# A two-layer decoder trunk on one core: gate and score orders, a three-block first gate load, and output weights taken early

## The chip, the core and the metric

The kernel runs on one core of a Trainium2 chip. A core has a matrix engine (TensorE, PE in the rows; PEld is its weight load), VectorE (DVE), ScalarE (ACT), GpSimd (POOL) and SyncE (SP), each with its own instruction queue that is worked off in order. Sixteen DMA engines move data for all of them. The metric is device time of the whole program in microseconds. A measurement of this kernel varies by about 0.2% (the three runs of before lie between 2964.33 and 2970.5 us).

## The reference

512 tokens of width 1024 pass two layers in float32. Layer 1 mixes tokens with gated linear attention (6 heads) and attention into 256 memory tokens; layer 2 with stick-breaking attention (12 heads) and the same memory attention. After each mixer comes an output projection, `x <- LN(alpha*x + mix)`, and then a product-key expert network (PEER), which holds most of the work:

```
s = einsum('nhpd,hpkd->nhpk', q, subkeys)            # 8 heads, 2 halves, 128 keys each
top_s, top_i = top_k(s, 16)                          # per half
best_s, best_pos = top_k(all 16*16 sums, 16)         # 16 experts of 16384 per token and head
g = softmax(best_s)
act = gelu(einsum('nd,nhkd->nhk', x, u_tab[idx]))
out = einsum('nhk,nhkd->nd', g * act, v_tab[idx])
x <- LN(alpha*x + out)
```

## The kernel before

Every float32 product is made of three fast ones: an operand is split into a high part (`hi`, ScalarE copy) and the rest (`lo`, VectorE subtraction), and TensorE adds hi·hi, hi·lo and lo·hi (`split` at L85, `stat_mm` at L106). A weight block of 128x1024 is loaded by SyncE's queue into one of four `raw` buffers, split into one of three `hl` buffers, and used for 24 matmuls.

Mixer A runs L395 to L640. The first blocks give the low-rank gate input `glr`; `gate_logits` (L444) multiplies it with a weight of 16 rows (tile `pz`) and takes Abs, Exp and Ln on ScalarE; keys, queries and values follow. `to_cat` (L547) transposes a head's result (tile `ptc`) and splits it into `cat`. `out_proj_ln` (L232) splits eight blocks of output weights (`woh`, `wol`), multiplies `cat` by them for four groups of 128 tokens (tile `oacc`), and normalizes. `warm_sqrt` (L917) is a one-element square root that loads ScalarE's table early. Mixer B (L647) ends in the same `out_proj_ln`; `phase3` and `phase4` are its last attention steps.

`peer` (L966) has two long phases for 384 of the 512 tokens. The first (U) makes 16 query blocks and their scores (`pq`, copied to `qT`, then `pss`; L1317 to L1350), then runs over 128 blocks of 128 experts: 24 matmuls give `ph`, ScalarE's Gelu gives the activations. All but the last KEEP=20 activations go to DRAM (`Ad`). Beside this, generators paced by a budget per block pick the experts of one token tile after the other (`rest`, L1288: `rows` is the top-k, then `indices`, `softmax`, `gate_prep`) and turn them into a dense gate matrix in DRAM (`Gd`). The other 128 tokens are handled by gathers: GpSimd fetches expert rows, VectorE multiplies (`gr`, `va`; stream `gus`).

The second phase (V) takes the experts in the order of `vorder`, the kept ones first: gate times activation gives `w` (L1423), split into `whi` and `wlo`, and 18 matmuls per block add into `acc`. Gates come from `Gd` in loads of several blocks. The first load has G0=1 block and lies in `big`, beside the kept activations; the second (3 blocks) lies in `xlo` and the third (8 blocks) in `xhi`, which are free only when the last matmul of U has read them. The later ones have 8 blocks and alternate between the two. All are issued by SyncE.

In U and V the order on PE, DVE and ACT is that of the code; in the mixers a scheduler orders ACT and DVE, and the code orders PE. A semaphore wait holds back all that stands behind it on that engine's queue, DMA issues included.

## Time and profile before

| | us |
|---|---|
| median of three runs | 2969.97 (2964.33 to 2970.5) |
| the profiled execution | 2965.86 |
| its span, first to last instruction | 2964.2 |
| TensorE busy | 2910.8 (98%) |
| VectorE busy | 2400.5 (81%) |
| ScalarE busy | 1429.6 (48%) |
| GpSimd busy | 640.8 (22%) |

Mixer A with its output projection fills the first 0.26 ms, PEER of layer 1 runs to 1.48 ms, mixer B to 1.75 ms, PEER of layer 2 to the end. TensorE has little idle time that the profile names, but a busy share says nothing about its clock: the columns of granted clock by stretch show where the engine worked at half speed. In the rows, `[1.63 <-ACT woh L98]` means that the engine sat idle for 1.63 us until ScalarE's instruction of line 98 was done.

### The profile page before, as it was taken

The page shows a single profiled execution, that of the slowest core. Times are in us where ns is not written, and L with a number is a line of the kernel's source. Part 1 is how long each engine was busy: PE and PEld are TensorE (multiplying, and loading weights), DVE is VectorE, ACT ScalarE, POOL GpSimd, SP SyncE. Part 2 cuts the span into 40 slices and gives each one's busy share as a digit, 9 for nine tenths or more (in the row PEclk, how much of TensorE's full clock was granted, in tenths as well). Part 3 has the DMA queues.
Part 4 walks back from the last instruction along what each step waited for, and adds up shares of the span by engine and source line. Part 5 has one row for each costly group of instructions (what it writes and reads, how often), then busy time and mean ns, then how long its engine had stood idle before and what let it go on. Part 6 is the DMA issues. An engine that isn't in the chain of part 4 may idle for free.

```text
span 2964.2 us, 44555 instructions
## 1 busy us (share of the span) xinstructions
PE 2910.8 (98%) x16274; PEld 2573.2 (87%) x16274; DVE 2400.5 (81%) x5301; ACT 1429.6 (48%) x2484; POOL 640.8 (22%) x560
## 2 busy tenths in 40 slices
PE   8999999999999999999999999999999999999998
PEld 7878899999998888888776788999999998888886
DVE  5556899999886888878967668999999778888888
ACT  5342357666674333333345523476676743333332
POOL 0100132221333222322002001312223233222220
PEclk9999999999999999999999999999999999999999
DMA  4331488889989999999511214888989999999995
GB/s 164 121 114 57 148 301 302 319 310 332 337 317 334 323 346 346 359 360 356 186 65 43 100 57 142 295 305 314 315 318 332 328 330 338 349 347 356 367 351 175
DMA packets 315132, 789.91 MB, mean 266 GB/s; under 512 B 41873, under 2 KB 134049, under 8 KB 308513
## 3 DMA queue, kind: packets, MB, share of 16 engines
q1 hardware_dynamic: 216960, 419.48, 41.1%
q0 software_dynamic: 73728, 268.47, 25.5%
q10 hardware_dynamic: 24224, 99.13, 8.5%
q8 instruction: 127, 2.08, 0.3%
q14 instruction: 93, 0.75, 0.1%
HBM read 692.09 MB, written 94.90 MB: 266 GB/s over the span
## 4 chain that ended last, share of the span: by engine, by line
PE 91%; DVE 6%; issue 1%; DMA 1%; ACT 1%; DVEq 0%; ACTq 0%; SPq 0%
PE ph L118 11%; PE ph L120 11%; PE ph L119 11%; PE acc L262 11%; PE acc L264 11%; PE acc L266 11%; PE pq L118 2%; PE pq L119 2%; PE pq L120 2%; PE pg L1274 1%; PE pg L1275 1%; PE pss L1322 1%; PE oacc L264 1%; PE oacc L266 1%; PE oacc L262 1%
## 5 line engine op out<-in xcount | busy, mean ns | idle before, releaser
L118 PE MATMUL ph<-xhi,uh 128*128 128x384 f32 x2048 | 700.7, 342 | 0.0
L120 PE MATMUL ph<-xhi,ul 128*128 128x384 f32 x2048 | 686.2, 335 | 0.2
L119 PE MATMUL ph<-xlo,uh 128*128 128x384 f32 x2048 | 685.3, 335 | 0.0
L98 ACT ACTIVATE vh<-vr 128x1024 fp32r<-128x1024 f32 x256 | 271.4, 1060 | 593.0 <-issue 401.3
L1002 POOL DMA_INDIRECT gr<-in_un,gidx x256 | 302.3, 1181 | 1010.7 <-DVE gr L1037 805.5
L262 PE MATMUL acc<-vh,whi 128*128 128x512 f32 x1536 | 474.8, 390 | 7.8 <-ACT whi L1426 7.8
L264 PE MATMUL acc<-vl,whi 128*128 128x512 f32 x1536 | 474.4, 390 | 0.0
L266 PE MATMUL acc<-vh,wlo 128*128 128x512 f32 x1536 | 473.7, 390 | 0.5 <-DVE wlo L1427 0.5
L1002 POOL DMA_INDIRECT gr<-in_vt,gidx x256 | 287.2, 1122 | 766.4 <-DVE va L1055 657.4
L99 DVE TENSOR_TENSOR vl<-vr,vh 128x1024 fp32r<-128x1024 f32 x256 | 313.2, 1224 | 170.3 <-ACT vh L98 170.0
L98 ACT ACTIVATE uh<-ur 128x1024 fp32r<-128x1024 f32 x288 | 304.6, 1058 | 245.3 <-PE ph L119 230.1
L99 DVE TENSOR_TENSOR ul<-ur,uh 128x1024 fp32r<-128x1024 f32 x288 | 350.0, 1216 | 68.0 <-ACT uh L98 65.2
L119 PEld LDWEIGHTS ph<-xlo,uh 128*128 128x128 f32 x2048 | 385.7, 188 | 0.0
L120 PEld LDWEIGHTS ph<-xhi,ul 128*128 128x128 f32 x2048 | 385.0, 188 | 0.8 <-DVE ul L99 0.8
L118 PEld LDWEIGHTS ph<-xhi,uh 128*128 128x128 f32 x2048 | 385.5, 188 | 0.0
L262 PEld LDWEIGHTS acc<-vh,whi 128*128 128x128 f32 x1536 | 288.0, 188 | 69.8 <-ACT whi L1426 10.4
L266 PEld LDWEIGHTS acc<-vh,wlo 128*128 128x128 f32 x1536 | 288.2, 188 | 61.7 <-DVE wlo L1427 2.2
L264 PEld LDWEIGHTS acc<-vl,whi 128*128 128x128 f32 x1536 | 288.3, 188 | 61.4 <-DVE vl L99 1.8
L1055 DVE SCALAR_TENSOR_TENSOR va<-gr,gw,va 128x1024 f32<-128x1024 f32 x254 | 324.8, 1279 | 13.1 <-DMA gr<-in_vt,gidx 12.8
L1037 DVE SCALAR_TENSOR_TENSOR gr<-gr,xnat 128x1024 f32<-128x1024 f32 x256 | 309.7, 1212 | 16.0 <-DMA gr<-in_un,gidx 15.9
L1247 ACT ACTIVATE obl<-obh,rat 128x128 f16<-128x128 f16 x768 | 244.3, 393 | 19.9 <-ACT gt L1278 6.1
L1426 ACT ACTIVATE whi<-w 128x384 fp32r<-128x384 f32 x256 | 130.9, 511 | 55.6 <-DVE w L1423 55.5
(332 smaller groups left out, 4136.5 us busy)
## 6 DMA issues: line engine op xcount, KB each, us to landing
ur<-in_ut SPq DMA_DIRECT2D x256, 512.0 KB
vr<-in_vt SPq DMA_DIRECT2D x256, 512.0 KB
Gd<-gt ACTq DMA_DIRECT2D x48, 1024.0 KB
gl<-Gd SPq DMA_DIRECT2D x30, 1536.0 KB
Ad<-act ACTq DMA_DIRECT2D x108, 384.0 KB
al<-Ad SPq DMA_DIRECT2D x108, 384.0 KB
ur<-in_wq SPq DMA_DIRECT2D x32, 512.0 KB
bs<-in_b_st SPq DMA_DIRECT2D x14, 512.0 KB
```

The costliest lines, as they stand in the source:

```text
L98: nc.scalar.activation(hi, raw, AF.Copy)
L99: sub = lambda: eng.tensor_sub(lo, raw, hi.bitcast(F32))
L118: nc.tensor.matmul(ps, h, xhi[:, c, sl], start=(c == 0), stop=False)
L119: nc.tensor.matmul(ps, h, xlo[:, c, sl], start=False, stop=False)
L120: nc.tensor.matmul(ps, l, xhi[:, c, sl], start=False, stop=(c == NC - 1))
L262: nc.tensor.matmul(acc[hf], lh, hi[:, hf * 512:(hf + 1) * 512], start=first, stop=False)
L264: nc.tensor.matmul(acc[hf], lh, lo[:, hf * 512:(hf + 1) * 512], start=False, stop=False)
L266: nc.tensor.matmul(acc[hf], ll, hi[:, hf * 512:(hf + 1) * 512], start=False, stop=last)
L1002: nc.gpsimd.indirect_dma_start(out=gr, out_offset=None, in_=tab, in_offset=bass.IndirectOffsetOnAxis(ap=gidx[:, k:k + 1], axis=0))
L1037: nc.vector.scalar_tensor_tensor(gr, gr, 1.0, E.x[:, 0], op0=ALU.mult, op1=ALU.mult, accum_out=gh[:, k:k + 1])
L1055: nc.vector.scalar_tensor_tensor(va, gr, gw[:, k:k + 1], va, op0=ALU.mult, op1=ALU.add)
L1247: nc.scalar.activation(obl[:, q], obh[:, q], AF.Copy, scale=rat[:, n0 + q:n0 + q + 1])
```

## The change

1. `gate_logits` yields after each of its three products, and one of them is made after each projection block instead of three in a row.
2. The output weights of mixer A's first two chunks, and of mixer B's first, are split before `out_proj_ln`, into buffers that are free by then (tags `za` and `zs`). The load of `x` for the first normalization is issued earlier.
3. `warm_sqrt` reads the LayerNorm weight `gam`, times zero, so it runs after that load has landed.
4. In the score loop the copy of a query block (`query`) is separated from its scores and made in the iteration in which the block is computed.
5. `rest` does one step of the next tile's top-k before `gate_prep` of the present one. The gather stream takes no step in the last two rounds of U.
6. KEEP goes from 20 to 18 and G0 from 1 to 3. The second gate load, now 7 blocks (3 to 9), is issued on ScalarE's queue; the third (10 to 17) stays on SyncE's.

The Python lines that carry the change (some buffer widths, and the buffer count of the LayerNorm's `lny`, are left out):

```diff
-def out_proj_ln(E, cat, wo, lng, lnb, ahead, order=range(NC), rows=None):
+def wo_split(E, wo, c, pool, tag="", rows=None):
+    return split(E, load_raw(E, wo[c], "wo"), "wo", pool, tag, rows=None if rows is None or c >= GH else rows[:, c:c + 1])
+def out_proj_ln(E, cat, wo, lng, lnb, ahead, order, w, rows=None):
...
     with E.tc.tile_pool(name="lp", bufs=1, reuse_waits="tile") as lp:
-        w = {}
         for c in order:
-            w[c] = split(E, load_raw(E, wo[c], "wo"), "wo", lp, f"wo{c}", rows=None if rows is None or c >= GH else rows[:, c:c + 1])
+            if c not in w:
+                w[c] = wo_split(E, wo, c, lp, f"wo{c}", rows)
         gam, bet = load_ln(E, lp, lng, lnb)
-        warm_sqrt(E)
+        warm_sqrt(E, gam)
         next(ahead)
...
     with tc.tile_pool(name="acat", bufs=1, reuse_waits="tile") as ap:
-        hgc = ap.tile([P, GH], F32, name="hgc")
+        hgc = ap.tile([P, 32], F32, name="hgc")
         kk = ap.tile([P, 8, T], F32, tag="kk", name="kk")
...
         cat[7] = c7[:, 0], c7[:, 1]
+        new_za = lambda name, shape=(2, T), dt=F32: ap.tile([P, *shape], dt, tag="za", name=name, bufs=4)
+        wo = {}
         for c in (4, 5):
...
             nc.scalar.dma_start(bgt, a["a_bg"])
-            nc.scalar.dma_start(hgc, a["a_hg"])
+            nc.scalar.dma_start(hgc[:, :GH], a["a_hg"])
             nc.gpsimd.memset(seg, 1.0)
...
                     nc.tensor.matmul(pz, w2[:, j], glr[:16], start=True, stop=True)
-                    za = wk.tile([P, 2, T], F32, tag="za", name="za", bufs=3)
+                    za = new_za("za")
                     zb, az = za[:, 0], za[:, 1]
...
                     zz.append((zb, az))
+                    yield
                 for zb, az in zz:
...
                 st = stat_units(E, wst, range(1, 9), ev_stat, name="as")
-                next(st)
-                gate_logits()
+                logits = gate_logits()
                 for _ in st:
-                    pass
+                    next(logits, None)
                 mhi, mlo = mem_split(E, mp, "mr", a["memT"])
...
                 mem = mem_attn(E, wk, qm, cat, lambda hh: wk.tile([P, NT, 256], F32, tag="S", name="mp"),
-                               lambda hh: wk.tile([P, 2, T], F32, tag="za", name="mpT", bufs=3), ptags=("ps", "ps", "ps"))
+                               lambda hh: new_za("mpT"), ptags=("ps", "ps", "ps"))
...
                 nc.gpsimd.tensor_copy(E.Vm, kv1[1])
+                nc.sync.dma_start(E.x, a["x"].rearrange("(t p) d -> p t d", p=P))
                 rg = mp.tile([P, NT, GH * P], F32, tag="mr", name="rg")
...
                 next(rs_)
+                for c in range(2):
+                    wo[c] = wo_split(E, a["a_wo"], c, lambda name: new_za(name, (D,), F32R), rows=hgc)
                 to_cat(2)
...
                     to_cat(h)
-                with tc.issue_after(E.last_load.ins):
-                    nc.sync.dma_start(E.x, a["x"].rearrange("(t p) d -> p t d", p=P))
         yield
-        out_proj_ln(E, cat, a["a_wo"], a["lng0"], a["lnb0"], E.ahead, [0, 1, 2, 3, 6, 7, 4, 5], hgc)
+        out_proj_ln(E, cat, a["a_wo"], a["lng0"], a["lnb0"], E.ahead, [0, 1, 2, 3, 6, 7, 4, 5], wo, hgc)
...
             new_cat(c)
+        new_zs = lambda name, n, dt=F32: cp.tile([P, n], dt, tag="zs", name=name, bufs=2)
         with tc.tile_pool(name="mbx", bufs=1, reuse_waits="tile") as mp, tc.tile_pool(name="mbwk", bufs=2, reuse_waits="tile") as wk:
...
                 for h in two:
-                    tiles[h] = (wk.tile([P, 1280], F32, tag="zs", name="zs", bufs=4),
+                    zs = wk.tile([P, 1280], F32, tag="zs", name="zs") if g % 4 else new_zs("zs", 1280)
+                    tiles[h] = (zs,
                                 wk.tile([P, 1280 + 3 * P], F32, tag="ez", name="ez", bufs=2))
...
                 phase3(11)
+                first = {0: wo_split(E, wo, 0, lambda name: new_zs(name, D, F32R))}
                 phase4(5)
         yield
-        out_proj_ln(E, cat, wo, lng, lnb, E.ahead, [0, 1, 2, 3, 4, 6, 7, 5])
+        out_proj_ln(E, cat, wo, lng, lnb, E.ahead, [0, 1, 2, 3, 4, 6, 7, 5], first)
...
-def warm_sqrt(E):
-    E.nc.scalar.activation(E.junk1, E.one1, AF.Sqrt)
+def warm_sqrt(E, after):
+    E.nc.scalar.activation(E.junk1, after[:, 0:1], AF.Sqrt, scale=0.0)
...
 T0 = T - TD
-KEEP = 20
+KEEP = 18
 KB = P - KEEP
...
 GD = 1
-G0 = 1
+G0 = 3
 VE = 8
...
             def rest():
+                prev = None
                 for k, t in enumerate(order):
...
                     sel = sels[k] if k < 2 else Sel(t)
-                    yield from sel.rows()
+                    rows = sel.rows()
+                    if prev:
+                        yield next(rows)
+                        yield from prev.gate_prep()
+                    yield from rows
                     yield from sel.indices()
                     yield from sel.softmax()
-                    yield from sel.gate_prep()
+                    prev = sel
+                yield from prev.gate_prep()
...
-            def scores(r, pq):
+            def query(pq):
                 qT = wk.tile([P, T], F32, tag="act", name="qT")
                 nc.scalar.activation(qT, pq, AF.Copy)
+                return qT
+            def scores(r, qT):
                 pss = psum(E, name="pss")
...
                 stat_mm(E, pes[r], *parts.pop(r), sl=LATE)
-            pq = None
+            qT = None
             for r in range(17):
...
                 if r > 0:
-                    ev = scores(r - 1, pq)
+                    ev = scores(r - 1, qT)
                 if r + 2 >= LEAD:
                     prep(r + 2)
+                if r < 16:
+                    qT = query(pn)
                 if r > 0:
                     ev()
-                pq = pn
                 if r > 1:
...
                     work(WB if ready else WB0)
-                gus(GU if work.q else GU2)
+                if b < P - 1:
+                    gus(GU if work.q else GU2)
                 if LOG:
...
         vorder = list(range(KB, P)) + list(range(KB))
+        def new_gates(i, i1):
+            return E.xp.tile([P, NSUB, i1 - i, TS], F32, tag=("xhi", "xlo")[gcuts.index(i) % 2], name="gl")
+        def load_gates(eng, dst, b, b1):
+            eng.dma_start(dst, Gd[:, :, b:b1].rearrange("s p i n -> p s i n"))
...
                     vp["g"] = g0
+                    load_gates(nc.sync, g0, b, b + g1)
+                elif i == G0:
+                    vp["g"] = vp.pop("second")
                 else:
-                    vp["g"] = E.xp.tile([P, NSUB, g1 - i, TS], F32, tag=("xhi", "xlo")[gcuts.index(i) % 2], name="gl")
-                nc.sync.dma_start(vp["g"], Gd[:, :, b:b + g1 - i].rearrange("s p i n -> p s i n"))
+                    vp["g"] = new_gates(i, g1)
+                    load_gates(nc.sync, vp["g"], b, b + g1 - i)
                 vp["i"] = i
...
             vprep(1)
+            vp["second"] = new_gates(G0, gcuts[2])
+            load_gates(nc.scalar, vp["second"], KB + G0, KB + gcuts[2])
             for b in range(P):
...
                     vp["ln"] = load_ln(E, wv, lng, lnb)
-                    warm_sqrt(E)
+                    warm_sqrt(E, vp["ln"][0])
                 gus(vb)
...
         if out_dram is None:
```

What stands where on the engines, before and after, at three places. A row is line, operation, written tile <- read tiles, shape; ACT, SP are queues worked off from top to bottom. Lines of after are those of the changed file.

**End of mixer A, ScalarE's queue.** `arh` and `rg` belong to the gated attention, `aT` and `sq` to a head's result, `cat` and `xhi` are what the output projection multiplies with, `woh` its weights, `uh` the first block of the expert network. Before, from the last transposes on:

```order
L192 ACTIVATE cat_1567<-ptc 128x512 x2
L609 ACTIVATE rg<-ara 128x256 x4
L192 ACTIVATE cat_1567<-ptc 128x512 x2
L192 ACTIVATE xhi<-ptc 128x512 x2
L101 ACTIVATE woh<-wo,hgc 128x1024 x4
L924 DMA gam<-in_lng 128x1024
L98 ACTIVATE woh<-wo 128x1024
L925 DMA bet<-in_lnb 128x1024
L98 ACTIVATE woh<-wo 128x1024
L101 ACTIVATE woh<-wo,hgc 128x1024 x2
L98 ACTIVATE uh<-ur 128x1024 x3
```

After, an earlier stretch (weights of the first two chunks):

```order
L100 ACTIVATE arh<-ar 128x1024
L194 ACTIVATE cat_102<-mo 128x512
L100 ACTIVATE arh<-ar 128x1024 x2
L103 ACTIVATE woh<-wo,hgc 128x1024
L100 ACTIVATE arh<-ar 128x1024
L103 ACTIVATE woh<-wo,hgc 128x1024
L100 ACTIVATE arh<-ar 128x1024
L543 ACTIVATE aT_608<-po 128x512
L545 ACTIVATE sq<-po 128x512
```

and from the last transposes on:

```order
L194 ACTIVATE cat_1567<-ptc 128x512 x2
L620 ACTIVATE rg<-ara 128x256 x4
L194 ACTIVATE cat_1567<-ptc 128x512 x2
L194 ACTIVATE xhi<-ptc 128x512 x2
L103 ACTIVATE woh<-wo,hgc 128x1024 x2
L100 ACTIVATE woh<-wo 128x1024 x2
L940 DMA gam<-in_lng 128x1024
L941 DMA bet<-in_lnb 128x1024
L103 ACTIVATE woh<-wo,hgc 128x1024 x2
L934 ACT_TABLE_LOAD
L934 ACTIVATE junk_70<-gam 128x1
L100 ACTIVATE uh<-ur 128x1024 x3
```

Two of the eight `woh` have moved ahead of the heads' results `aT` and `sq`; six remain behind the last `cat`, and the square root of `junk` now reads `gam`.

**Score loop, ScalarE's queue.** `qT` is the copy of a query block, `sall` that of its scores, `uh` the split of the next weights. Before:

```order
L1319 ACTIVATE qT<-pq 128x512
L98 ACTIVATE uh<-ur 128x1024
L1323 ACTIVATE sall<-pss 128x512
L1319 ACTIVATE qT<-pq 128x512
L98 ACTIVATE uh<-ur 128x1024
L1323 ACTIVATE sall<-pss 128x512
L1319 ACTIVATE qT<-pq 128x512
```

After:

```order
L1342 ACTIVATE qT<-pq 128x512
L100 ACTIVATE uh<-ur 128x1024
L1342 ACTIVATE qT<-pq 128x512
L1349 ACTIVATE sall<-pss 128x512
L100 ACTIVATE uh<-ur 128x1024
L1342 ACTIVATE qT<-pq 128x512
L1349 ACTIVATE sall<-pss 128x512
L100 ACTIVATE uh<-ur 128x1024
```

The copy `qT` of a block stands one weight split earlier: ahead of `sall` of the block before instead of behind it.

**Start of V, the queues that issue the gate loads.** `vr` are weight loads of V, `gl` gate loads (24x16 elements a block: 24x48 is three blocks, 24x112 seven, 24x128 eight). SyncE before, from the third-last weight load ahead of them:

```order
L86 DMA vr<-in_vt 128x1024 x3
L1411 DMA gl<-Gd 128x24x48
L1411 DMA gl<-Gd 128x24x128
L86 DMA vr<-in_vt 128x1024 x2
L1411 DMA gl<-Gd 128x24x128
L86 DMA vr<-in_vt 128x1024 x8
L1411 DMA gl<-Gd 128x24x128
```

SyncE after:

```order
L85 DMA vr<-in_vt 128x1024 x3
L1432 DMA gl<-Gd 128x24x128
L85 DMA vr<-in_vt 128x1024 x7
L1432 DMA gl<-Gd 128x24x128
L85 DMA vr<-in_vt 128x1024 x8
L1432 DMA gl<-Gd 128x24x128
```

ScalarE before (`keep` is an activation of the last blocks of U, `vh` a weight split of V, `whi` the high part of gate times activation):

```order
L98 ACTIVATE vh<-vr 128x1024
L1366 ACTIVATE keep<-ph 128x384
L1426 ACTIVATE whi<-w 128x384
L98 ACTIVATE vh<-vr 128x1024
L1366 ACTIVATE keep<-ph 128x384 x2
L1426 ACTIVATE whi<-w 128x384
L98 ACTIVATE vh<-vr 128x1024
L1426 ACTIVATE whi<-w 128x384
L98 ACTIVATE vh<-vr 128x1024
```

ScalarE after:

```order
L1393 ACTIVATE keep<-ph 128x384
L100 ACTIVATE vh<-vr 128x1024
L1393 ACTIVATE keep<-ph 128x384
L1463 ACTIVATE whi<-w 128x384
L100 ACTIVATE vh<-vr 128x1024
L1393 ACTIVATE keep<-ph 128x384
L1463 ACTIVATE whi<-w 128x384
L1432 DMA gl<-Gd 128x24x112
L1393 ACTIVATE keep<-ph 128x384
L100 ACTIVATE vh<-vr 128x1024
L1463 ACTIVATE whi<-w 128x384
```

The second gate load has left SyncE's queue, grown from three blocks to seven, and stands in ScalarE's behind the second `whi`; the load of eight blocks is now the first of the two in SyncE's queue. The first gate load lies outside these rows (earlier in SyncE's queue); it has three blocks instead of one.

## Rows read from the trace of the kernel before

**Rows 1.** Page: span, busy time, costliest group (busy, mean ns, idle before).

```profile
span 2964.2 us, 44555 instructions
...
PE 2910.8 (98%) x16274; PEld 2573.2 (87%) x16274; DVE 2400.5 (81%) x5301; ACT 1429.6 (48%) x2484; POOL 640.8 (22%) x560
...
L99 DVE TENSOR_TENSOR vl<-vr,vh 128x1024 fp32r<-128x1024 f32 x256 | 313.2, 1224 | 170.3 <-ACT vh L98 170.0
```

**Rows 2.** Waits of TensorE over the span: us in total, times, longest.

```profile
PE acc L262 <- ACT whi L1426: 7.8, 6, 4.5
...
PE pss L1322 <- ACT qT L1319: 4.7, 4, 1.2
PE gtp L1209 <- DVE best L1183: 3.8, 2, 1.9
```

**Rows 3.** Chain that ended last: start us, us, what.

```profile
15.70 0.23 PE asp L118
...
21.83 3.17 PE pz L447 x6
...
30.43 0.43 PE asp L118
...
145.58 1.02 PE pd L507 x28
...
200.58 7.28 DMA wo<-in_a_wo
...
939.05 7.62 DMA gl<-Gd
...
2427.01 5.85 DMA gl<-Gd
```

**Rows 4.** Stretches: busy by engine, then PEclk, DMA share, GB/s.

```profile
24.90:31.00 6.10, 6.10 (x16) 4.77 (x15) 1.04 (x2) 6.04 (x9) 0.00 (x0) 0.51 0.26 86
140.00:183.00 43.00, 42.99 (x367) 34.86 (x367) 14.49 (x43) 14.11 (x21) 9.71 (x5) 1.00 0.29 104
945.00:950.00 5.00, 2.14 (x5) 1.75 (x6) 3.30 (x5) 2.11 (x4) 0.00 (x0) 0.57 1.08 312
950.00:955.00 5.00, 5.00 (x18) 3.97 (x18) 5.00 (x7) 1.89 (x3) 2.60 (x1) 0.75 1.09 346
2092.50:2096.00 3.50, 3.50 (x13) 3.50 (x12) 3.20 (x8) 3.07 (x5) 0.11 (x1) 0.51 0.49 187
```

**Rows 5.** Timeline of TensorE, projection A: start, us, instructions [idle before].

```profile
193.64 0.33 PE L550 MATMUL ptc<-ident,aT 128*128 128x128 f32 x1 [1.07 <-DVE aT L544]
195.70 1.22 PE L262 MATMUL oacc<-woh,cat 128*128 128x512 f32 x2 [1.72 <-ACT woh L101]
...
210.97 0.63 PE L266 MATMUL oacc<-woh,xlo 128*128 128x512 f32 x2
```

**Rows 6.** Timeline of TensorE, projection B.

```profile
1680.42 2.37 PE L750 MATMUL pav<-zs,v 128*64 128x512 f32 x14 [0.41 <-ACT zs L742]
1684.41 0.73 PE L262 MATMUL oacc<-woh,cat 128*128 128x512 f32 x2 [1.63 <-ACT woh L98]
...
1697.69 0.62 PE L266 MATMUL oacc<-woh,cat 128*128 128x512 f32 x2
```

**Rows 7.** Timeline of TensorE, starts of V in both layers.

```profile
939.03 0.63 PE L262 MATMUL acc<-vh,whi 128*128 128x512 f32 x2
...
942.70 0.61 PE L266 MATMUL acc<-vh,wlo 128*128 128x512 f32 x2
947.86 1.22 PE L262 MATMUL acc<-vh,whi 128*128 128x512 f32 x2 [4.55 <-ACT whi L1426]
...
2434.05 0.73 PE L262 MATMUL acc<-vh,whi 128*128 128x512 f32 x2 [1.96 <-ACT whi L1426]
```

**Rows 8.** Timeline of ScalarE, middle of V in layer 1.

```profile
1207.85 0.34 ACTq L924 DMA_DIRECT2D gam<-in_lng  x1
...
1211.52 1.06 ACT L98 ACTIVATE vh<-vr 128x1024 fp32r<-128x1024 f32 x1 [1.06 <-issue]
```

More of the change, by code (lines that the diff above doesn't have):

```diff
@@ L49, in setup @@
     E.Vm = E.cp.tile([P, 2, 256], F32, name="Vm")
-    E.one1 = E.cp.tile([P, 1], F32, name="one1")
+    E.pad1 = E.cp.tile([P, 1], F32, name="pad1")
     E.junk1 = E.cp.tile([P, 1], F32, name="junk1")
-    nc.gpsimd.memset(E.one1, 1.0)
     E.zl = E.cp.tile([1, P], mybir.dt.bfloat16, name="zl")
@@ L94, in split @@
     pool = pool or E.hl
-    hi = pool.tile([P, D], F32R, tag=tag + "hi", name=f"{name}h")
-    lo = pool.tile([P, D], F32R, tag=tag + "lo", name=f"{name}l")
+    if callable(pool):
+        hi, lo = pool(f"{name}h"), pool(f"{name}l")
+    else:
+        hi = pool.tile([P, D], F32R, tag=tag + "hi", name=f"{name}h")
+        lo = pool.tile([P, D], F32R, tag=tag + "lo", name=f"{name}l")
     if rows is None:
@@ L404, in mixer_a @@
             w2 = mp.tile([16, 3, P], F32, name="w2")
-            bgt = mp.tile([P, 3], F32, name="bgt")
+            bgt = mp.tile([P, 16], F32, name="bgt")[:, :3]
             msk = mp.tile([P, P], mybir.dt.uint8, name="msk")
@@ L890, in layer_norm @@
     nc = E.nc
-    y = lp.tile([P, D], F32, tag="lny", name="lny", bufs=2)
+    y = lp.tile([P, D], F32, tag="lny", name="lny")
     st = E.lnp.tile([P, 2, 6], F32, tag="lnst", name="lnst", bufs=2)
```

## The prediction

> **What bounds the kernel now.** I read the page first. TensorE is busy for 2910.8 of 2964.2 us [rows 1], so nothing else can bound the whole, and the change adds no product. What it can win is the 53 us in which TensorE is idle, and the time in which it counts as busy at half clock. So I read next the waits of TensorE, which name three that the change touches [rows 2]; then the chain of waits, for places where a DMA ended last [rows 3]; then the granted clock of the stretches behind those places [rows 4]; and last the timelines of TensorE around both output projections and the starts of V [rows 5 to 7], where a matmul's start says more than a sum of idle time. The reader is to see there that the losses are short and lie at seams: none is over 5 us of idleness, and most are followed by some us at clock 0.5.
>
> Everything is summed against the profiled execution, 2965.86 us. It is 4.1 us below the median of the three runs shown, 2969.97; I set the prediction between both.
>
> **Part by part.** (1) *Gate logits.* The six products `pz` stand together and take 3.17 us [rows 3], with 16 rows of the array in use. Behind them the clock is 0.51 (1.2 of 2.4 GHz) for 24.9 to 31.0 us, and a matmul of `asp` takes 0.43 instead of 0.23 us [rows 3, 4]. About 6.1 / 0.43 = 14 matmuls run there, less the one at the seam: 13 x 0.20 = 2.6, and 0.3 for the step itself, 2.9 us lost. Spread out, each pair is about 1 us long. A stretch of 28 small products of 1.02 us in all [rows 3] lies in 140 to 183 us, whose clock is 1.00 [rows 4]: so much does not make it fall there. Breaking the projection two more times I put at 0.25 each. I take -2.4, with ends of -2.9 and, if each of the three makes the clock fall as the six did, 3 x 2.9 - 2.9 = +5.8. ScalarE's table changes that this brings are hidden: the logits are used only in the keys, many blocks later.
>
> (2) *Output projection of A.* The last `ptc` ends at 193.64 + 0.34 = 193.98, and the 48 matmuls of the first four tiles' share run until about 211.43 [rows 5]: 17.45 us for 48 x 0.23 = 11.0 of work. So 6.4 us can be had. Two chunks ready at the start give 12 matmuls, 2.8 us, of cover for the third, whose two splits are then under way. But the last weight load still waits for a buffer and takes 7.28 us to land [rows 3], beside `gam`, `bet` and now no longer `x`. I take -5.0; ends -6.4 and -1.7, the last being the first wait alone, 1.72 [rows 5].
>
> (3) *Scores.* `pss` waits 4.7 us for `qT`, four times [rows 2]. With `qT` ahead of `sall` and made in the iteration of its own block, it has the whole score group to get done. -4.5; ends -4.7 and 0.
>
> (4) *Gate transposes.* `gtp` waits 3.8 us for VectorE's softmax, twice, and the clock behind one is 0.51 for 3.5 us [rows 2, 4], of which half, 1.7, is lost. With one step of the next tile's top-k set between the softmax and the transposes the wait goes in both. -4.5; ends -5.5 and 0, if VectorE, which is then later with the next weights (`ul`), gives it back.
>
> (5) *Output projection of B.* `pav` ends at 1682.79, the first half of the projection at 1697.69 + 0.46 = 1698.15 [rows 6]: 15.36 for 11.04 of work, 4.3 to be had. Only one chunk is ready here, so a later one may be short: -3.0; ends -4.3 and -1.0.
>
> (6) *Start of V.* Layer 1 waits 4.55 us after its first block, as its second gate load lands only at 946.7, 7.62 us after its buffer came free [rows 3, 7]. The clock then falls to 0.57 and 0.75 [rows 4]: 0.43 x 2.14 + 0.25 x 5 = 2.2 lost. So 6.8 in all; layer 2 loses 1.96. Afterwards the first load covers three blocks. A block is 18 x 0.23 = 4.1 us [rows 7], so the fourth starts 12.3 us after 939.03, at 951.3, and VectorE and ScalarE need its gates 1.2 us before, at 950.1 (product and copy, the gap from 946.67 to 947.86). Its load has 24 x 112 x 4 x 128 bytes, 1.38 MB instead of 0.59, and cannot start before 939.05 either: `xlo` is read by the last product of U. It now runs beside the 1.57 MB of SyncE's eight-block load, not ahead of it, and beside two gathers of 0.52 MB. All four are 4.0 MB; at the 312 GB/s of [rows 4] they take 12.8 us, so it lands at 952 to 953 and TensorE waits 2 to 3 us, in both layers. With the clock behind it that is worth 2.7: layer 1 gains 4.1, layer 2 loses 0.8. I take -3. The ends: -8.8 if the load is in time, and +9.3 if it only gets the rate of the three-block load (0.59 MB in 7.62 us, 77 GB/s), as then it needs 17.8 us, lands at 956.9 and each layer loses 9.
>
> By the Trainium skill, page "DMA: Bandwidth & Descriptors", section "Issuing engines are not separate DMA queues", transfers issued by ScalarE, SyncE and GpSimd end on the same 16 engines and interleave, and issuing from several saves only the issue time. By that rule the two loads share the rate, as the sum above has them, and the move of the queue gains nothing and gives up the place ahead. Had ScalarE's queue engines of its own, the load would land about like the one of before, and term 6 would be -8.8. The row at 945 to 950, with every engine busy (DMA share 1.08), speaks for sharing.
>
> (7) *The square root.* In V it now waits for `gam`, and ScalarE's queue with it: the next `vh`, then `vl` on VectorE. That `vh` starts at 1211.52 and is multiplied two blocks later, 8.2 us; less 1.06 and 1.22 [rows 1, 8] 5.9 us are spare. `gam` is issued at 1207.85 [rows 8], so it may take 9.6 us to land. The landings shown take 5.85 to 7.62 us [rows 3]. I take 0; the end is rival 4.
>
> Two kept activations fewer mean two more to DRAM and back, 0.2 MB each way of 790 MB; the gather stream skips two rounds in U and has V to catch up, under TensorE's work. Both 0.
>
> Sum: -2.4 - 5.0 - 4.5 - 4.5 - 3.0 - 3.0 = -22.4. That is 2943.5 against the profiled execution, 2947.6 against the median; I say 2946.
>
> **The rivals.** *Seven blocks in time.* If the load of ScalarE's queue gets more than half of the rate, it lands by 950.1 and term 6 is -8.8: -28, 2939. For it speaks the 346 GB/s of the stretch behind [rows 4]; against it the queue's size.
>
> *A long wait at the fourth block.* If it gets the rate of the three-block load, term 6 is +9.3: -10, 2956. For it: that load too ran beside gathers and the eight-block one. Against it: that one was bound by what lay ahead of it at its start, and its rate need not hold for 1.38 MB.
>
> *Waits replaced.* The clock falls at each gate product (+5.8), or VectorE's late `ul` takes the place of the transposes' wait, and the third chunk of both projections is as late as the first was: -10 again, 2956. For it speaks that six products of 3.17 us did it once; against it the 1.00 over 43 us with such stretches [rows 4].
>
> *Slower: the square root holds V up.* ScalarE stands still until `gam` is there, and with it the splits of weights and gates. Up to 9.6 us nothing happens; beyond that each us costs one, in both layers. To use up 22.4 us it must take 9.6 + 11.2 = 20.8 us to land. At 25 us each layer loses 15.4 and some 2 of clock: +35, so +13 in all, 2979. For it: `gam` stands in a row with gathers that fill the engines all through V. Against it: loads of the same size landed in 6 to 8 us under that load.
>
> *Nothing moves.* The waits named are parts of 53 us of idleness, and each could be the front of another one, so that about nothing is left, 2966.
>
> **How the numbers follow.** Forecast 0.50, seven blocks in time 0.22, a long wait 0.15, waits replaced 0.08, square root 0.03, nothing 0.02. The range reaches from below the second case, 2933 (all terms near their good ends), to above the third and fourth, 2961. It leaves out the last two and the tails. Faster or slower counts from 0.2%, 6 us, about what a measurement of this kernel can tell: below 2964, within, above 2976. The forecast and its first three rivals, 0.95 together, lie below 2964; I leave 0.07 of that to their upper tails, so faster 0.88; same 0.08, six of those seven and the last case; slower 0.04, the square root and the rest.
>
> **What the new profile would show.** (1) `pz` in three pieces and clock 1.00 behind each; (3, 4) no `pss` and hardly a `gtp` among the waits; (2, 5) the first `oacc` within 0.5 us of the last `ptc` and `pav`, and both first halves near 11 to 13 us; (6) the wait of `acc` for `whi` gone from the second block and at the fourth, 2 to 3 us in both layers, landing of the second load 13 to 14 us after the last product of U; (7) ScalarE idle before `junk`, TensorE not waiting. Wrong it would be most of all by a fourth block that waits 6 us or not at all, by a clock under 1 in the projection after the products, or by an idle TensorE in the middle of V.

## The result and the profile after

Median 2946.44 us of four runs (2942.42 to 2950.92) against 2969.72 (2964.33 to 2970.5): ratio 0.9926, 95% interval 0.9905 to 0.9946, so faster by 16 to 28 us. 2946 was forecast. The profiled execution took 2949.05 us, so the two profiles differ by 16.8, less than the medians do (23.3).

The page of the changed kernel, beside [rows 1]:

```profile
span 2947.4 us, 44587 instructions
...
PE 2901.4 (98%) x16274; PEld 2566.8 (87%) x16274; DVE 2400.9 (81%) x5301; ACT 1435.6 (49%) x2486; POOL 654.1 (22%) x559
```

The busy time of TensorE fell by 9.4 us with the same number of matmuls, mostly time at half clock (the stretches at half clock ahead of the last `acc` add up to 27.3 us before and 10.2 after); its idle time fell from 53.4 to 46.0 us. Its waits, beside [rows 2] (us in total, times, longest):

```profile
PE acc L269 <- ACT whi L1463: 11.0, 6, 4.9
```

`pss` and `gtp` are gone from this view. `acc` waits more than before, 11.0 instead of 7.8 us. The chain that ended last, beside [rows 3]:

```profile
20.88 1.05 PE pz L457 x2
21.93 0.43 PE asp L120
22.36 0.24 PE asp L121
...
926.36 16.08 DMA gl<-Gd
...
2406.02 16.15 DMA gl<-Gd
```

The products `pz` stand in pairs of 1.05 us, with one slow matmul behind a pair, then 0.24. The second gate load of V takes 16.1 us in both layers (before 7.62 and 5.85). Stretches, beside [rows 4] (busy by engine, clock, DMA share, GB/s):

```profile
20.80:45.00 24.20, 24.20 (x98) 17.79 (x98) 15.65 (x19) 21.13 (x29) 0.00 (x0) 1.00 0.49 174
...
926.40:942.40 16.00, 12.38 (x55) 9.89 (x53) 4.18 (x4) 2.91 (x4) 2.80 (x2) 1.00 1.11 333
944.00:949.00 5.00, 5.00 (x17) 3.99 (x17) 5.00 (x7) 2.00 (x3) 1.01 (x1) 0.73 0.54 147
```

The clock stays at 1.00 behind the logits; at the start of V the DMA engines are full until the second load has landed (share 1.11), and a clock of 0.73 follows the wait. The timeline of TensorE, beside [rows 5 to 7]:

```profile
190.71 0.33 PE L561 MATMUL ptc<-ident,aT 128*128 128x128 f32 x1 [1.06 <-DVE aT L555]
190.81 0.71 PE L269 MATMUL oacc<-woh,cat 128*128 128x512 f32 x2
...
1667.25 2.37 PE L764 MATMUL pav<-zs,v 128*64 128x512 f32 x14 [0.40 <-ACT zs L756]
1669.54 0.73 PE L269 MATMUL oacc<-woh,cat 128*128 128x512 f32 x2
...
1680.35 0.73 PE L269 MATMUL oacc<-woh,cat 128*128 128x512 f32 x2 [0.74 <-ACT woh L100]
1681.61 0.73 PE L271 MATMUL oacc<-wol,cat 128*128 128x512 f32 x2 [0.53 <-DVE wol L101]
...
943.63 1.22 PE L269 MATMUL acc<-vh,whi 128*128 128x512 f32 x2 [4.85 <-ACT whi L1463]
...
2423.36 1.22 PE L269 MATMUL acc<-vh,whi 128*128 128x512 f32 x2 [4.92 <-ACT whi L1463]
```

Both projections start right behind the last transpose and the last `pav`. In that of B the wait has moved to the seventh of the eight chunks. In V it has moved from the second block to the fourth, 4.85 and 4.92 us. ScalarE in the middle of V, beside [rows 8]:

```profile
1194.71 0.35 ACTq L940 DMA_DIRECT2D gam<-in_lng  x1
...
1203.47 0.20 ACT L934 ACTIVATE junk<-gam 128x1 f32<-128x1 f32 x1 [6.41 <-DMA gam<-in_lng]
```

`gam` lands 8.8 us after its issue (9.1 in layer 2); ScalarE idles for 6.41 us, and TensorE does not wait.

Where the time went is best read by taking the same matmul in both traces (same tile, same place in TensorE's order) and subtracting its start times. The difference steps only where one kernel loses time and the other doesn't:

| matmul | before | after | difference | step | part |
|---|---|---|---|---|---|
| first `pz` | 21.76 | 20.81 | -0.95 | -0.95 | start |
| `asp` behind the products | 38.70 | 35.29 | -3.41 | -2.5 | (1) |
| last `ptc` of A | 193.64 | 190.71 | -2.93 | +0.5 | |
| `oacc`, second token tile | 211.44 | 204.08 | -7.36 | -4.4 | (2) |
| last `pss`, layer 1 | 352.52 | 342.38 | -10.14 | -2.8 | (3) |
| first `acc`, layer 1 | 939.03 | 926.34 | -12.69 | -2.6 | (4) |
| `acc`, 26 us on | 965.11 | 951.97 | -13.14 | -0.4 | (6) |
| last `pav` | 1680.42 | 1667.25 | -13.17 | 0.0 | |
| `oacc`, end of first tile | 1697.69 | 1683.57 | -14.12 | -1.0 | (5) |
| last `pss`, layer 2 | 1838.90 | 1822.04 | -16.86 | -2.7 | (3) |
| end of U, layer 2 | 2426.99 | 2405.99 | -21.00 | -4.1 | (4) |
| `acc`, 18 us on | 2444.79 | 2427.79 | -17.00 | +4.0 | (6) |
| last `acc` | 2953.17 | 2936.36 | -16.81 | +0.2 | |

The step at the start is not the change's. The first matmuls come 0.43 us apart until 13.6 us before and until 11.4 us after, and 0.23 us apart from then on, as they do at half and at full clock; over the thirteen profiles of this document that change comes anywhere from 11.1 to 13.9 us, with either order of the products. The +0.5 between the products and the last `ptc` stands in all seven profiles of the changed kernel and its variants (0.45 to 0.48) and in no other; what it is was not traced.

### The profile page after: what moved, and what is told of

The parts are those of the page before. It is cut to its first block, busy times and chain, and to the rows that moved or that the text cites. A ratio compares the mean times of both kernels' runs of the same rounds, so it can differ in the third digit from the quotient of the medians.

```text
span 2947.4 us, 44587 instructions
## 1 busy us (share of the span) xinstructions
PE 2901.4 (98%) x16274; PEld 2566.8 (87%) x16274; DVE 2400.9 (81%) x5301; ACT 1435.6 (49%) x2486; POOL 654.1 (22%) x559
## 4 chain that ended last, share of the span: by engine, by line
PE 93%; DVE 4%; DMA 2%; ACT 1%; issue 1%; DVEq 0%; ACTq 0%; SPq 0%
PE ph L120 12%; PE ph L122 12%; PE ph L121 12%; PE acc L269 11%; PE acc L271 11%; PE acc L273 11%; PE pq L121 2%; PE pq L120 2%; PE pq L122 2%; PE pg L1290 2%; PE pg L1291 1%; DMA gl<-Gd 1%; PE pss L1348 1%; PE oacc L271 1%; PE bsp L120 1%; PE bsp L121 1%
## 5 line engine op out<-in xcount | busy, mean ns | idle before, releaser
L1018 POOL DMA_INDIRECT gr<-in_vt,gidx x256 | 298.9, 1168 | 758.5 <-DVE va L1071 658.5
L269 PEld LDWEIGHTS acc<-vh,whi 128*128 128x128 f32 x1536 | 288.5, 188 | 73.2 <-ACT whi L1463 13.6
```

Of the source, the lines that this page charges most:

```text
L269: nc.tensor.matmul(acc[hf], lh, hi[:, hf * 512:(hf + 1) * 512], start=first, stop=False)
L1018: nc.gpsimd.indirect_dma_start(out=gr, out_offset=None, in_=tab, in_offset=bass.IndirectOffsetOnAxis(ap=gidx[:, k:k + 1], axis=0))
```

## The experiments

"The alignment" below is this subtraction; where no other kernel is named, it is from the first profile of the kernel before. Ratios are to the kernel before, with 95% intervals; the runs of before beside these kernels had medians of 2966.8 to 2967.6.

**V's start as before, in the changed kernel.**

```diff
-KEEP = 18
+KEEP = 20
...
-G0 = 3
+G0 = 1
...
-                elif i == G0:
-                    vp["g"] = vp.pop("second")
...
-            vp["second"] = new_gates(G0, gcuts[2])
-            load_gates(nc.scalar, vp["second"], KB + G0, KB + gcuts[2])
```

> The changed kernel with V's start as before (20 kept blocks, a first load of one block, a second of three on SyncE). Theory A: in the changed kernel's profile the starts of V lose 4.85 and 4.92 us of waits and, by the granted clock, 1.7 and 3.4 us behind them, 14.9 us, where the kernel before lost 8.8; so taking this part back gains about 6: 2943 against 2949 for the profiled run, ratio to the changed kernel 0.998. Rival B (the prediction's term of -3 holds and the profiled run was an untypical one): 3 us slower than the changed kernel.

2942.39 us, ratio 0.9911 (0.9897 to 0.9925). That is 4 us less than the changed kernel in the medians (not run side by side) and 6.7 in the spans. The intervals of the two ratios overlap, so the medians alone don't show it; the alignment of the two profiles does. The starts of V are shorter by 4.2 us in layer 1 (from the first `acc` on, 21.5 us for what took 25.6) and by 4.6 in layer 2, 8.8 in all, and some 2 us are lost again around projection B, where the clock falls in this profile and not in the changed kernel's. Theory A held, and rival B, 3 us slower, is ruled out: none of the five runs is over 2943.7. The chain shows one thing more: the old three-block loads now land after 5 us, where they took 7.62 and 5.85.

```profile
926.64 5.00 DMA gl<-Gd
...
2404.01 5.25 DMA gl<-Gd
```

Something else in the change speeds these loads up; the ninth experiment finds it.

**The second load on SyncE's queue.**

```diff
-            load_gates(nc.scalar, vp["second"], KB + G0, KB + gcuts[2])
+            load_gates(nc.sync, vp["second"], KB + G0, KB + gcuts[2])
```

> The changed kernel with the seven-block load on SyncE's queue, ahead of the eight-block load. Theory A (the two loads alternate packet by packet, so each has half the rate): in one queue it has nothing but the gathers beside it and lands 8 to 10 us after the last product of U instead of 16.1; gates are needed after 11.1 us, so the wait of acc at the fourth block and the low clock behind it go in both layers: 13 to 15 us, 2935. Rival B (the load's own size in packets of 448 bytes is the bound): it lands after 13 us or more, a wait of 2 us or more stays, 2941 or more.

2935.32 us, ratio 0.9887 (0.9872 to 0.9903). From 927 to 933 us the DMA queues (packets, MB, share of the 16 engines) and the gate loads (KB, us to landing) read:

```profile
q1 hardware_dynamic: 2887, 1.76, 99.7%
...
gl<-Gd SPq DMA_DIRECT2D x1, 1536.0 KB, 12.4
gl<-Gd SPq DMA_DIRECT2D x1, 1344.0 KB, 8.7
```

The 1344-KB load lands after 8.7 us, with the eight-block load (1536 KB) behind it in one queue, issued 5.6 us later. Of the waits of `acc` this is left:

```profile
PE acc L269 <- ACT whi L1463: 1.3, 4, 0.4
```

In the changed kernel the two loads stand in two queues, q1 (SyncE) and q10 (ScalarE). From 930 to 936 us:

```profile
q1 hardware_dynamic: 1858, 0.95, 61.3%
q10 hardware_dynamic: 1883, 0.84, 58.7%
```

They take turns, 1858 packets and 1883 (in each us some 310 of either), and get 0.95 and 0.84 MB: each has about half of the rate. Theory A is shown: only the queue was changed here, so the size alone is not the bound.

**The second load cut in two (three blocks on ScalarE's queue, four on SyncE's).**

```diff
-        gcuts = [0, G0] + [i for i in range(G0 + 1, P) if (i - KEEP) % GB == 0] + [P]
+        gcuts = [0, G0, 6] + [i for i in range(G0 + 1, P) if (i - KEEP) % GB == 0] + [P]
```

> The changed kernel with the second load cut in two: three blocks on ScalarE's queue, then four on SyncE's, then eight as before. Theory A (bytes in flight at the start set the landing): 0.59 MB beside 0.79 MB instead of 1.38 beside 1.57 land 7 to 9 us after the last product of U, before the 11.1 us, no wait in either layer, 2935. Rival B (the gathers hold the last packets, whatever the size): it lands at 12 us or later and 1 us or more of wait stays.

2935.45 us, ratio 0.9888 (0.9873 to 0.9903). VectorE's first product with these gates starts 9.7 and 9.3 us after the load's issue (934.98 - 925.25, 2408.78 - 2399.48), a little later than expected, and `acc` waits 1.5 us in all, at most 0.4 at once. Theory A held again: fewer bytes beside the gates do what the other queue does. Not only the cut does that: the eight-block load, whose buffer the three blocks now hold, is issued only at 942.1 us and has left the start of V. These two kernels beat both others, the changed one by 11 us (the intervals of the ratios, 0.9872 to 0.9903 and 0.9905 to 0.9946, do not overlap).

**No gathers in the first five blocks of V.**

```diff
-                gus(vb)
+                if b >= 5:
+                    gus(vb)
```

> The changed kernel, but the gather stream takes no step in the first five blocks of V. Theory A (4-KB packets of the gathers come between the last small packets of the seven-block load): it lands 11.5 to 13 us after the last product of U instead of 16.1, the waits fall from 4.9 to 0.5 to 2 us, 6 to 12 us in all, if the gathers catch up. Rival B (the two gate loads alone set it): it lands after 15 to 16 us as now and the waits stay at 4 to 5 us.

2957.59 us, ratio 0.9963 (0.9949 to 0.9977): slower than the changed kernel by 11. Theory A had set a condition, that the gathers catch up, and it was not met. The loads land sooner,

```profile
925.57 13.93 DMA gl<-Gd
...
2415.77 12.76 DMA gl<-Gd
```

by 2.2 and 3.4 us of the 16.1, so the gathers do hold them, as the queues of the changed kernel show from 938.0 to 942.3 us, the last 4.3 before the landing:

```profile
q0 software_dynamic: 258, 0.93, 55.6%
q1 hardware_dynamic: 519, 0.67, 43.8%
q10 hardware_dynamic: 32, 0.01, 1.1%
```

32 packets of the gate load (q10) trickle between 258 of the gathers (q0). But 13.9 and 12.8 us are left, in which few gathers run (104 of 6582 packets in layer 1, issued in U): there the two gate loads and the weight loads fill the DMA engines. And the gathers do not catch up in V of layer 1 (waits of TensorE, then a stretch at its end):

```profile
PE xtp L894 <- DVE xnat L929: 9.7, 1, 9.7
...
PE acc L269 <- ACT whi L1463: 4.9, 4, 2.7
```

```profile
1440.00:1456.00 16.00, 6.31 (x21) 5.32 (x21) 14.21 (x31) 1.60 (x4) 0.00 (x0) 0.57 0.08 29
```

TensorE waits 9.7 us for the tokens that the gathers serve, at clock 0.57 around it; the alignment has 12.4 us lost there. In layer 2 the time from the last `acc` to the end is 4.7 us longer (15.7 against 11.0), as VectorE comes to the gathered tokens' normalization 23 us later (2929.3 against 2906.0). So V's gather stream has no five blocks to spare.

**LayerNorm weights behind the output weights.**

```diff
-        gam, bet = load_ln(E, lp, lng, lnb)
-        warm_sqrt(E, gam)
+        with E.tc.issue_after(E.last_load.ins):
+            gam, bet = load_ln(E, lp, lng, lnb, nc.sync)
+        warm_sqrt(E, w[order[-1]][0].bitcast(F32))
...
```

> The changed kernel, but in both output projections the loads of the LayerNorm weights go through SyncE's queue, behind the last output weights, and the early square root reads the last woh instead of gam. Theory A (1 MB of these weights shares the DMA engines with the last four output-weight loads, so that these land 5.6 us after issue): the last loads take 3.5 us or less, the waits of oacc in projection B (2.5 us, clock included, at the sixth and the seventh chunk) shrink by 1.5 to 2 us; total 1.5 to 2.5 us less than the changed kernel. Rival B (the loads wait for raw buffers, which the splits free one by one): landing and waits as now, total within 0.5 us of the changed kernel's without V's start.

2949.82 us, ratio 0.994 (0.9927 to 0.9954). The alignment with the changed kernel shows a gain of 0.4 us through projection B (and 0.9 through A), both within what the variants of the changed kernel scatter there; 1.5 to 2 were expected in B, and the load that ends the chain there takes 5.5 us:

```profile
1675.02 5.48 DMA wo<-in_b_wo
```

Theory A fell. The last four loads are issued one by one, each when a split has freed its `raw` buffer (in the changed kernel at 1669.4, 1672.5, 1673.6 and 1674.8), and lie behind each other in SyncE's queue. That buffers and not only the queue set it was not tried.

**`gam` loaded three times in V.**

```diff
                     vp["ln"] = load_ln(E, wv, lng, lnb)
+                    for _ in range(2):
+                        nc.scalar.dma_start(vp["ln"][0], lng.partition_broadcast(P))
```

> The changed kernel with the load of gam in the middle of V made three times, each waiting for the one before, so that the square root is held for some 3 x 8.7 = 26 us after the first issue instead of 8.7. The prediction's account of the square root (up to 9.6 us of landing nothing happens, beyond it each us costs one in each layer, and the clock falls behind): TensorE idle for 16 us in each layer and 2 to 3 us lost at low clock, 36 to 39 us over the changed kernel. Rival (ScalarE's backlog is worked off before TensorE needs it, so that more than 9.6 us is to spare): 25 us or less.

2973.47 us in one run, 24.4 over the profiled run of the changed kernel. That is the rival's number, but for another reason: the later loads were shorter, and the hold was 20.0 us (1215.24 - 1195.28), not 26. The chain and ScalarE:

```profile
1195.28 9.01 DMA gam<-in_lng
...
1204.36 7.11 DMA gam<-in_lng
...
1211.49 3.73 DMA gam<-in_lng
```

```profile
1215.24 0.20 ACT L934 ACTIVATE junk<-gam 128x1 f32<-128x1 f32 x1 [2.10 <-DMA gam<-in_lng]
```

TensorE in both layers:

```profile
1216.85 1.22 PE L269 MATMUL acc<-vh,whi 128*128 128x512 f32 x2 [9.84 <-ACT whi L1463]
...
2709.63 1.22 PE L269 MATMUL acc<-vh,whi 128*128 128x512 f32 x2 [10.04 <-ACT whi L1463]
```

It is idle for 9.84 us at a hold of 19.96, and for 10.04 at 20.17. If each us beyond what is to spare costs one, as the prediction has it, 10.1 us are to spare, where the prediction had 9.6; one length of hold can't show the two apart. With the low clock behind the waits the alignment loses 12.4 and 12.1 us a layer, 24.7 in all. The changed kernel's own 8.8 and 9.1 us leave 1.0 to 1.3 of the 10.1.

**The score loop alone, on the kernel before.**

```diff
...
-                    ev = scores(r - 1, pq)
+                    ev = scores(r - 1, qT)
                 if r + 2 >= LEAD:
                     prep(r + 2)
+                if r < 16:
+                    qT = query(pn)
                 if r > 0:
                     ev()
-                pq = pn
```

> The kernel before with the new order of the score loop alone. Theory A (the waits of pss for qT and the restart of TensorE behind each of them): in the alignment of TensorE's instructions 2.7 to 2.8 us are gained in each layer's score loop, 5.5 in all, and no wait of pss is left; ratio 0.998. Rival B (the gain seen in the changed kernel's score loop is partly that of another edit): 4.7 us, the waits of before, or less.

2962.32 us, ratio 0.9982 (0.9973 to 0.9991). No wait of `pss` is left, and the alignment gains 2.8 us in the score loop of each layer, 5.5 in all. Theory A held.

**Top-k ahead of the gate transposes alone, on the kernel before.**

```diff
+                prev = None
                 for k, t in enumerate(order):
...
-                    yield from sel.rows()
+                    rows = sel.rows()
+                    if prev:
+                        yield next(rows)
+                        yield from prev.gate_prep()
+                    yield from rows
...
-                    yield from sel.gate_prep()
+                    prev = sel
+                yield from prev.gate_prep()
```

> The kernel before with the new order of top-k and gate transposes alone (the gather stream goes on as before). Theory A (waits of gtp, restarts and the clock behind the second): 2.6 us are gained in U of layer 1 and 4.2 in U of layer 2, 6.9 in all, with no low clock in layer 2's U. Rival B (VectorE's late ul takes some back, or part of the gain belongs to the skipped gathers): 4 us or less.

2958.99 us, ratio 0.9974 (0.9964 to 0.9984). The alignment gains 2.6 us in layer 1 and 4.3 in layer 2, and no low clock is left in U. Theory A held.

**The skipped gathers alone, on the kernel before.**

```diff
-                gus(GU if work.q else GU2)
+                if b < P - 1:
+                    gus(GU if work.q else GU2)
```

> The kernel before, but the gather stream takes no step in the last two rounds of U. Theory A (gathers issued there are still in flight at the start of V and delay the second gate load; with V's start as before but the skip in place it landed after 5.0 us, in the kernel before after 7.62): landing 5 us, wait of at most 2.3 us and no low clock at the start of V of layer 1, 4 to 5 us gained there, nothing in layer 2; total -4 to -5. Rival B (the landing varies from run to run and kernel to kernel with where the gathers happen to stand): waits of 4 us or more in one layer, total within 2 us of before.

2960.88 us, ratio 0.9977 (0.9968 to 0.9986). The second gate load, and the waits of `acc`:

```profile
939.61 4.94 DMA gl<-Gd
...
2424.09 4.99 DMA gl<-Gd
```

```profile
PE acc L262 <- ACT whi L1427: 5.1, 6, 1.9
```

The alignment gains 4.7 us at V's start in layer 1 and nothing that lasts in layer 2. Theory A held: with the skip this load landed after 4.94, 4.99, 5.00 and 5.25 us (here and in the first experiment), without it after 5.72 to 8.50 (eight landings in four profiles of kernels with the old start). That layer 2 gains nothing is the draw of the first profile: the three others without the skip lose 1.4, 3.8 and 5.4 us more than it at that place, and in layer 1 they differ from it by 1.1 at most. Against the mean of the four the skip is worth 4.5 us in layer 1 and 2.1 in layer 2, near the 6 us between the medians.

**The new start of V alone, on the kernel before.** The edit is part 6 of the change.

> The kernel before with V's start of the changed kernel alone (18 kept blocks, first load of three, seven blocks on ScalarE's queue). Theory A (both loads at half rate, last packets behind gathers): the wait at the fourth block is 4.5 us or more in both layers, with low clock behind it; 3 to 7 us slower than before. Rival B (the prediction's term): 3 us faster than before, landing 13 to 14 us after the last product of U.

2975.48 us, ratio 1.0030 (1.0018 to 1.0042): slower by 5 to 12 us. Waits and landings:

```profile
PE acc L262 <- ACT whi L1435: 17.9, 6, 8.6
```

```profile
934.12 8.05 DMA gr<-in_vt,gidx
...
943.46 0.56 DVE w L1432
...
944.05 0.01 ACT whi L1435
944.06 16.54 DMA gl<-Gd
...
2435.77 17.34 DMA gl<-Gd
```

TensorE waits 8.07 and 8.55 us at the fourth block, more than in the changed kernel. The landing takes only 0.5 and 1.2 us longer; what is added is that the load is issued late, 3.8 and 3.9 us after the first `acc` (940.27 and 2431.86), where the changed kernel issues it with the first `acc` (926.36 and 926.34). It stands behind the second `whi` in ScalarE's queue, `whi` waits for VectorE's `w`, and VectorE for a gather of U's last rounds, as the rows show. Theory A held in kind; its size was too small.

**The kernel before, once more.**

> The kernel before, unchanged, profiled once more. Theory A (whether the clock falls behind a short idle time or behind the six logit products differs from execution to execution; two kernels with the same first 30 us showed 3.4 and 0 us of low clock there instead of 6.8): the stretches of low clock are not the same five as in the first profile, above all behind the logits. Rival B (they belong to the program): the same stretches of 6.8, 6.8, 6.8, 3.4 and 3.4 us at the same places.

2966.35 us, nearly the profiled time of the first profile, but not made of the same losses. Behind the six products, where [rows 4] has 0.51:

```profile
24.00:31.00 7.00, 7.00 (x31) 5.74 (x31) 1.64 (x4) 6.79 (x10) 0.00 (x0) 1.00 0.24 77
```

The same stretch in the two kernels that change only the scores, and only the gate transposes:

```profile
24.00:31.00 7.00, 7.00 (x25) 5.56 (x25) 1.65 (x4) 6.85 (x10) 0.00 (x0) 0.76 0.25 77
```

```profile
24.00:31.00 7.00, 7.00 (x33) 5.73 (x32) 1.65 (x4) 6.94 (x11) 0.00 (x0) 1.00 0.21 75
```

The kernel with the new start of V alone has 0.76 there, that with the skipped gathers alone 1.00 (25 to 32 us). So six profiles with the products in a row have 0.51, 0.76 twice and 1.00 three times; the seven with the products apart, the changed kernel's and those of its variants, all have 1.00 there. The kernel before also had its second load of V land after 6.93 and 8.21 us this time. Theory A held. Why the clock falls in one execution and not in the next stays open.

## Why the prediction came out right, and which of its steps did not

The median was met to 0.5 us, by errors that cancel in part and by luck: the forecast stood between two references 4 us apart, and the sum of -22.4 stands against -16.8 between the profiles and -23.3 between the medians.

(1) Logits: -2.5 in the profiles, -2.4 forecast. The low clock behind the products is gone in all seven profiles of the new order, but the price was one draw: half of the profiles with the old order lose nothing there. Over the six, the mean loss is 1.1 us (0.49 of 6.1 us once, 0.24 of 7 us twice, nothing three times). And the new order costs something by itself: from the first `pz` to the `asp` behind the products it takes 14.5 us in all seven, and the three old ones without low clock take 13.8. Against the mean of the six the change is worth 0.4 us, so the met number is luck.

(2) Projection A: -4.4 for -5.0 (-4.4 to -5.3 in the seven profiles with the change). Right.

(3) Scores: -5.5 for -4.5, past the end given (-4.7). The waits alone were counted. A wait is counted from the end of the last matmul's record; the records of `pss` are 0.28 us long and start every 0.11 us, so some 0.2 us of what each wait costs is not in its number.

(4) Gate transposes: -6.7 for -4.5, past the end of -5.5, and shown alone as -6.9. The waits went whole, and nothing came back as a late `ul`, for which 1 us had been held off. What goes beyond 5.5 was not traced; the uncounted 0.2 us of each wait can be a part.

(5) Projection B: -1.0 for -3.0, its upper end. As suspected a later chunk is short: by their issue times the loads behind the fourth wait for buffers. A wait at the first chunk became one at the seventh.

(6) Start of V: the step that failed. It was to bring -3. By the table both starts of V cost 3.6 (-0.4 and +4.0), and that is already with what the skipped gathers bring; with the skip in both kernels the term costs 8.8 (the first experiment), and alone 5 to 12. The sentence "they take 12.8 us, so it lands at 952 to 953" took bytes over rate. The rate was near, 333 GB/s for 312. The bytes were not: up to the landing 5.33 MB moved instead of 4.0 (packets, MB and share of the queues from 926.4 to 942.4 us):

```profile
q1 hardware_dynamic: 3380, 2.61, 54.3%
q10 hardware_dynamic: 3088, 1.38, 34.7%
q0 software_dynamic: 375, 1.34, 22.1%
```

SyncE's queue (q1) moved 2.61 MB, of which the eight-block load is 1.57; the rest, 1.04, are weight loads, which the sum left out. The gathers (q0) moved 1.34 where it had 1.05. So the landing without gathers, after 12.8 and 13.9 us, does not bear the sum out: 4.37 MB moved there in layer 1, weight loads among them. Within the 16.1 us the two queues took turns. By the Trainium skill, page "DMA: Bandwidth & Descriptors", section "Issuing engines are not separate DMA queues", they were to interleave; this trace agrees, with 1858 packets against 1883. Then the gathers' packets held the last ones back, which made up 2.2 and 3.4 us of it. The wait is 4.9 instead of 2 to 3 us, in both layers, and low clock follows (0.73 over 5 us in layer 1, 1.4 us lost; 0.50 over 4.6 us in layer 2, 2.3 lost). The rival of a long wait was nearer for this term (+9.3 of it, from 17.8 us).

What hid the failure is the skipped gathers, put at 0: against the first profile they are worth 4.7 us in layer 1, because it is their transfers that delayed the old load, and some 2 more in layer 2 against the mean of four profiles. That the stream "has V to catch up" was right; what it no longer does at the seam was not looked at.

(7) The square root: 0, as forecast, with 0.5 to 0.8 us left by the prediction's spare time and 1.0 to 1.3 by the measured one. The rival of a blocked ScalarE has its rule right to 0.5 us at a hold of 20, and its condition was not met.

That the profiled executions differ by 16.8 and the medians by 23.3 is within what the runs scatter: the four runs of the changed kernel are 2942, 2944, 2949 and 2951. The profiled one has long waits at V in both layers, and the first profile of before has the shortest start of V in layer 2 of the four without the skip. Whether the two quick ones had shorter ones wasn't seen, as they have no trace.

## What to carry to other kernels

A load that moves to another engine's queue loses its place in line: ahead of a load in one queue it landed first here, beside it both landed late. And it takes over what its new queue waits for (3.8 us with the new start of V alone). So count, for a load at a seam, all bytes that move until it lands, weight loads and gathers issued before the seam among them, and keep what is needed first small or first. And before a loss of a few us is given a price, look for it in a second profile of the same program: the waits for an engine's order came back to 0.1 us here, landings and the low clock did not.

## What the runs showed of the chip that was not expected

- Two queues with small packets shared about packet by packet (1858 of 512 bytes against 1883 of 448 in 6 us); the last 32 packets of one took about 4 us between 4096-byte packets of the gathers.
- Behind the same six matmuls the granted clock was 0.51, 0.76 or 1.00 in different executions (over 6 to 7 us).
- The same 512-KB load, made three times in a row on one queue, landed after 9.01, 7.11 and 3.73 us.
